# A two-layer hybrid decoder trunk: where weights, replicated rows and transfers are put, and how the planner counts transfers

## The chip, the cores and the metric

One core of one Trainium2 chip runs the whole kernel. The metric is the device time of one launch in microseconds; less is better. The kernel before took 3025.5 us (median of three runs, 3023.38 to 3030.99). The engines are named as the profile names them: PE (TensorE matmul) with PEld (its weight load), DVE (VectorE), ACT (ScalarE), POOL (GpSimd), SP (SyncE). SPq and ACTq are the instruction queues of SyncE and ScalarE seen as issuers of transfers.

## The reference

The input is x, 2048 tokens of 1024 channels, float32. Layer 0 is a gated DeltaNet, layer 1 gated linear attention, each followed by `layer_norm(alpha*x + y)`.

- Gated DeltaNet, 8 heads with 128 key and 256 value channels: one projection of x gives q, k, v, a gate and two logits a head. q, k and v pass a causal convolution over 4 tokens and SiLU, q and k are normalised. In each block of tokens (64 in the reference) a lower triangular system `(A + I) U = [beta*v, beta*k*exp(gc)]` is solved, with `A` the strictly lower part of `beta*k k^T` times a decay. A state of 128 x 256 is then carried from block to block: `v_new = u - w S`, `o = q_dec S + qk v_new`, `S = S*g_last + k_dec^T v_new`.
- Gated linear attention, 4 heads of the same widths: a decay per channel from a low-rank gate, products q k^T with that decay within a block, and a state carried on in the same way.
- Both: the head's output is RMS-normalised, multiplied by `norm_w * silu(gate)`, and goes through an output projection.

## The kernel before, in words

**Staging.** The tokens are cut into 4 groups of 512 (`TG`), and a group into 4 chunks of 128 (`NC`). A unit is one head of one layer for one group: 32 DeltaNet units and 16 units of the second layer, in the order of `PHASES`. Each unit has four stages: `gemms` (input projections), `preps` (decays, products and the triangular solve), `chains` (the state over four chunks), `outs` (output projection, layer norm).

**Weights.** A matmul in full precision is made of three in a reduced format: a float32 weight is split into a high and a low part. `chunk` (line 508) loads a raw block of 128 rows (`wraw`, 6 buffers), ACT copies the high part and POOL subtracts to get the low part, both into a tile `wc` of shape `[P, 2, 272]` with 9 buffers. Units after the second store the split block in device memory (`wk`), and later units load it back with one transfer `wc<-wk`. Most blocks are 256 columns wide, so that the two parts lie 272 elements apart in a partition: two pieces of 1 KB.

**The triangular solve.** `gdn_prep` (line 800) writes the four diagonal 32 x 32 blocks of A of each chunk into `own` (tile `X0`), stores them in device memory, and reads them back replicated: each row of a block is wanted in all the 32 partitions of that block. Two stores, `blk` (all columns) and `blkq` (the first 16 of each 32), are issued by ACT. Then SyncE issues eight loads into `Arep`: four of rows 16 to 31 (256 KB each, one a block of 32 partitions), and four of rows 0 to 15 cut to 16 columns (128 KB each). DVE then goes through the rows from 31 down to 1, two instructions a row (`Xt<-Arep,X` and `X<-X,Xt`, line 861). `Arep` has one buffer.

**Transfers by queue.** SyncE issues all loads and most stores. ACT issues five kinds: `gcT` and `Gb` (the decays of a head, stored and read back in all partitions), `blk`, `blkq`, and `x2T` (the transposed output of layer 0). A transfer instruction is issued in the order of its queue. It counts up one of eight semaphores, numbers 100 to 107 in the trace, that the two queues share: an instruction whose semaphore still belongs to an earlier transfer, on either queue, waits until that one has landed.

**What sets the order.** Nothing is run while it is recorded: `Recorder.note` (line 133) notes each instruction with its dependencies, `cost` (line 183) gives it a busy time and a lag, and `place` (line 234) is a list scheduler. It keeps a clock for each engine, takes the ready instruction of highest priority (chains, preps, early preps, outs, gemms, layer norm, setup; `R_CHAIN` and so on in line 1185), gives out buffers, and so fixes the order of every engine's instructions. `emit` writes them in that order; on the chip each engine follows its list and waits by semaphores. The planned times decide the order alone.

For transfers the planner before has fixed figures: the issue takes 630 ns for `wc` and `wk`, 560 for `wraw`, 430 for `Arep`, 480 for the others, and 340 on ACT; the data is there 3500 ns plus its size at 170 bytes a nanosecond later, 7000 ns for `Arep`, 9500 for `y` and `woraw`. No transfer delays another, apart from the issue time.

Of the kernel before, what the change touches and what calls it, by code (L numbers as in the profile page):

```python
# [7 lines left out]
F32 = mybir.dt.float32  # L8
F32R = mybir.dt.float32r
# [3 lines left out]
ALU = mybir.AluOpType  # L13
# [3 lines left out]
P = 128  # L17
# [3 lines left out]
TG = 512  # L21
NG = SEQ // TG
NC = TG // P
# [84 lines left out]

class Op:
    __slots__ = ("key", "call", "name", "args", "kw", "prio", "cost", "lag", "deps", "users", "waits", "ready",  # L110
                 "views", "fresh", "start", "at", "func", "unit")


def size_of(shape):
# [6 lines left out]
class Recorder:  # L121
# [61 lines left out]
    def cost(self, op, dst, every):  # L183
        key = op.key
        n = size_of(dst.shape)
        psum = any(isinstance(a, View) and a.of.psum for a in every)
        op.func = None
        if key == "t":
            mov = size_of(every[2].shape) if op.name == "matmul" else size_of(every[1].shape)
            if op.name == "transpose":  # L190
                op.cost = 2 * dst.shape[0] / 2.4 + 4
            elif every[1].dtype == F32:
                op.cost = 2 * max(mov / 1.2 + 3, 0.85 * every[1].shape[-1] + 2)
            else:
                op.cost = mov / 2.25 + 4.5
            op.lag = 210
            op.func = op.name == "matmul" and min(dst.shape[0], every[1].shape[0]) < P
        elif key == "d":
            size = 4 * n * dst.shape[0]
            tag = dst.of.tag if isinstance(dst, View) else ""  # L200
            op.cost, op.lag = 630 if tag == "wc" or tag[:2] == "wk" else 560 if tag == "wraw" else 480, DMA_LAG + size / 170
            if tag == "Arep":
                op.cost, op.lag = 430, REP_LAG
            elif tag in ("y", "woraw"):
                op.lag = 9500
        elif key == "a":
            size = 4 * n * dst.shape[0]
            op.cost, op.lag = 340, DMA_LAG + size / 170 + (2500 if isinstance(every[1], View) and every[1].of.tag == "xraw" else 0)
        elif key == "v":
            n = max(n, max(size_of(a.shape) for a in every))  # L210
            took = (150 if psum else 160) + 1.04 * n
            if op.name in ("tensor_reduce", "copy_predicated", "tensor_tensor_scan"):
                took += 1.0 * n
            if op.name != "tensor_tensor" and any(isinstance(a, (View, bass.AP)) and size_of(a.shape) == 1
                                                  for a in every[1:]):
                took += 62 if psum or n < 512 else 85
            op.cost, op.lag = took - 80, 80 + LAG
        elif key == "s":
            took = (165 if psum else 210) + 0.833 * n
            if any(isinstance(op.kw.get(k), (View, bass.AP)) for k in ("scale", "bias")):  # L220
                took += 100 + 67 * ("scale" in op.kw and "bias" in op.kw)
            if "accum_out" in op.kw:
                took += 190
            if op.name == "activation":
                op.func = "ln" if op.args[2] == AF.Ln else None if op.args[2] in (AF.Copy, AF.Square, AF.Identity,
                                                                                 AF.Abs) else "exp"
            op.cost, op.lag = took - 95, 95 + LAG
        else:
            took = 140 + 2.8 * n if len(every) > 2 else 185 + n
            if op.args[-1] == ALU.pow:  # L230
                took = 450 + 160 * n
            op.cost, op.lag = took - 40, 40 + LAG

    def place(self):
# [4 lines left out]
        pending = {e: [] for e in clock}  # L239
# [12 lines left out]
            due[op.unit] += op.prio[0] == R_CHAIN  # L252
        front = 0

        def engine(op):
            return "s" if op.key == "a" else op.key

        def blocked(op):
            for t in op.fresh:
# [4 lines left out]
        def offer(op):  # L264
            tag = "unit" if op.fresh and op.unit > front + HORIZON else blocked(op)
            if tag is not None:
                parked.setdefault(tag, []).append(op)
                return
            ready = op.ready
            for t in op.fresh:  # L270
                ready = max(ready, min(free[t.tag])[0])
            heapq.heappush(pending[engine(op)], (ready, op.prio, op.at))

        def wake(tag):
            for op in sorted(parked.pop(tag, []), key=lambda o: o.prio):
# [6 lines left out]
        while len(placed) < len(self.ops):  # L282
# [16 lines left out]
            if blocked(op) is not None:  # L299
                clock[e] = now  # L300
                offer(op)
                continue
            late = max([0.0] + [min(free[t.tag])[0] for t in op.fresh])
            if late > now:
                heapq.heappush(pending[e], (late, op.prio, op.at))
                continue
# [19 lines left out]
            op.start = now  # L326
            clock[e] = now + cost
            busy[e] += cost
            end = now + cost + op.lag
            placed.append(op)  # L330
            for u in op.users:
                u.ready = max(u.ready, now + cost if u.deps[op] else end - LAG + DRAIN if u.key == op.key == "v" else
# [34 lines left out]
class Recorded:  # L367
# [2 lines left out]

    def __getattr__(self, name):
        def call(*args, also=(), behind=(), **kw):
            key = "a" if self.key == "s" and name == "dma_start" else self.key
            self.recorder.note(self.engine, key, name, args, kw, also, behind)
        return call


LAG, DRAIN = 60, 35
DMA_LAG, REP_LAG, SLACK = 3500, 7000, 100
INSPECT = None  # L380


# [1 line left out]
def trunk(ctx, tc, x, xT, w_in1, conv, a_log, dt_bias, nw1, w_out1, w_in2, gk_up, gk_b, nw2, w_out2,  # L384
# [1 line left out]
    nc = tc.nc  # L386
    rec = Recorder()
    v, s, g = (rec.engine(e, k) for e, k in ((nc.vector, "v"), (nc.scalar, "s"), (nc.gpsimd, "g")))
    pe, sync, acts = rec.engine(nc.tensor, "t"), rec.engine(nc.sync, "d"), s

    def pool(name, bufs=1, space=None):
        kw = {} if space is None else {"space": space}
# [115 lines left out]
    def chunk(spec):  # L508
# [1 line left out]

        w, cols, kc, key = spec
        keep = rec.unit >= N_UNKEPT
        wc = T("wc", [P, 2, 272], W_BUFS, F32R)
        n = sum(2 * cn if pair else cn for c0, cn, pair in cols)
        if key in kept:
            sync.dma_start(wc[:, :, :n].bitcast(F32), kept[key][:])
            return wc
        raw = T("wraw", [P, 272], RAW_BUFS)
        rows = w[kc * P:(kc + 1) * P]
# [8 lines left out]
                n += cn  # L528
        split(wc[:, 0, :n], wc[:, 1, :n], raw[:, :n], g)
        if keep:  # L530
            kept[key] = T("wk", [P, 2, n], p=dr)
            sync.dma_start(kept[key][:], wc[:, :, :n].bitcast(F32))
        return wc

    def load_wo(spec, parts=None):
# [82 lines left out]
    def flat(t):  # L618
        return t.rearrange("p a b -> p (a b)")
# [124 lines left out]
    def gdn_logits(G, gi):  # L744
# [40 lines left out]
        row = T("Gb", [P, TG])[:H1 * NC, :P]  # L785
        s.copy(row, dT)
        rows = T(f"gcT_{gi}", [H1 * NC, P], p=dr)
        acts.dma_start(rows[:], row)
        G.update(beta=beta, ngc=ngc, gdec=gl, eg=eg, rows=rows)

    def later_half(a, sz):
# [8 lines left out]
    def gdn_prep(u):  # L800
        h, G = u.h, u.G
        beta, ngc, eg = G["beta"][:, h, :], G["ngc"][:, h, :], G["eg"]
        Gb = T("Gb", [P, NC, P])
        acts.dma_start(flat(Gb[:]), G["rows"][h * NC:(h + 1) * NC, :].rearrange("a b -> (a b)").unsqueeze(0)
                            .broadcast_to([P, NC * P]))
        D1, D2 = T("D1", [P, NC, P], 2), T("D2", [P, NC, P], 2)
        for n in range(NC):
# [38 lines left out]
        for r0 in range(0, P, 32):  # L846
            r = slice(r0, r0 + 32)
            s.copy(own[r].rearrange("p (n j) -> p n j", n=NC), A[r, :, r])
        late, early = (T(f"{k}_{u.at}", [P, 32 // m * NC], p=dr) for m, k in ((1, "blk"), (2, "blkq")))
        acts.dma_start(late[:], own[:])  # L850
        acts.dma_start(early[:].rearrange("p (n j) -> p n j", n=NC), own[:].rearrange("p (n j) -> p n j", n=NC)[:, :, :16])
        R = T("Arep", [P, 3 * 16 * 16 * NC])
        n = 16 * 32 * NC
        for part, rows, c in ((late, slice(16, 32), slice(0, n)), (early, slice(0, 16), slice(n, 3 * n // 2))):
            for b in range(4):
                sync.dma_start(R[b * 32:(b + 1) * 32, c],
                               part[b * 32 + rows.start:b * 32 + rows.stop, :].rearrange("s n -> (s n)").unsqueeze(0)
                               .broadcast_to([32, c.stop - c.start]))
        X, xt = T("X", [P, NC, 32]), T("Xt", [P, NC, 31])
        g.tensor_copy(X[:], bc(id32[:], 1, NC))  # L860
        for q in range(31, 0, -1):
            w = 32 if q >= 16 else 16
            at = (q - 16) * w * NC if q >= 16 else n + q * w * NC
            row = R[:, at:at + w * NC].rearrange("p (n j) -> p n j", n=NC)[:, :, :q]
            v.tensor_tensor(xt[:, :, :q], row, X[:, :, q:q + 1].broadcast_to([P, NC, q]), ALU.mult)
            v.tensor_tensor(X[:, :, :q], X[:, :, :q], xt[:, :, :q], ALU.subtract)
        v.tensor_tensor(Tm[:].rearrange("p n (b j) -> p n b j", j=32), bc(X[:], 2, 4),
                        bc(C(C_BLK).rearrange("p (b j) -> p b j", j=32), 1, NC), ALU.mult)
# [22 lines left out]
    def gla_prep(u):  # L891
# [13 lines left out]
        kq = u.kq  # L905
        At = T("D2", [P, NC, P], 2)
        b3 = b.rearrange("p (n t) -> p n t", n=NC)
        near = T("Arep", [P, 3 * 16 * 16 * NC])[:, :2 * TG].rearrange("p (n k) -> p n k", n=NC)
        s.copy(near[:, :, :P], kq[:, 1])
        odd = near[:, :, P:P + P // 2]  # L910
        v.tensor_tensor(odd, b3[:, :, 1::2], b3[:, :, 0::2], ALU.subtract)
# [183 lines left out]
    def outs(u):  # L1095
# [40 lines left out]
        if u.last and u.kind == 0:  # L1136
            for kc in range(KC):
                d = PS("g", [P, NC, P])
                xt = T("xraw", [P, TG], X_RAW_BUFS)
                for n in reversed(range(NC)):  # L1140
                    pe.transpose(d[:, n, :], ys[n][:, kc * P:(kc + 1) * P], ident, also=(xt,) if n == NC - 1 else ())
                s.copy(xt[:], flat(d))
                acts.dma_start(x2T[u.gi][:, kc, :], xt[:])

    def load_gb(u, which):
        gb = {}
# [30 lines left out]


PS_BUFS = {"g": 3, "c": 3, "h": 1, "o": 1}
W_BUFS, RAW_BUFS, X_RAW_BUFS = 9, 6, 4  # L1180
WO_BUFS, WO_RAW_BUFS = 2, 2
LN_BUFS = 4
N_WARM = 5
# [46 lines left out]
```

## Time and profile before

| | |
|---|---|
| median of three runs | 3025.5 us |
| profiled execution | 3028.51 us, its span 3026.3 us |
| mean granted clock of TensorE | 0.988 |
| busy: PE, PEld, DVE, ACT, POOL | 97%, 80%, 73%, 41%, 17% of the span |
| transfers | 612.87 MB, mean 203 GB/s |

How to read the rows: a group's row ends with its number, its busy time and mean, and the idle time of the engine ahead of it with what ended it. `A <- B: 20.9, 14, 4.6` among the waits means that A waited for B 20.9 us in total, 14 times, at most 4.6 us. In a row of a stretch, `PE busy (x)` is the busy time with the number of instructions, then follow the granted clock (`PEclk`, 1.00 is full), the mean busy share of the 16 transfer engines, and what they moved. Nearly all rows name line 364, as the planner's `emit` writes all instructions there; the tiles tell them apart.

### The profile page before, as it was taken

How to read it: one execution, taken by the hardware profiler on the slowest of the kernel's cores; microseconds unless marked ns; L12 is line 12 of the kernel's file. 1: busy time of each engine (PE TensorE's matmuls, PEld its weight loads, DVE VectorE, ACT ScalarE, POOL GpSimd, SP SyncE). 2: the span in 40 equal slices, each digit the busy share in tenths (PEclk: the TensorE clock that was granted, in tenths of full speed). 3: DMA queues.
4: the chain of work that ended last, by engine and by line, in shares of the span. 5: the costliest groups of instructions: out<-in, count | busy, mean ns of one | idle time of the engine just before them, and what ended most of it. 6: DMA issues, size and time to landing. Idle time of an engine off the chain costs nothing. (4 is left out here: it accounts for less than half of the span.)

```text
span 3026.3 us, 48052 instructions
## 1 busy us (share of the span) xinstructions
PE 2926.2 (97%) x16172; PEld 2419.0 (80%) x16172; DVE 2201.4 (73%) x5374; ACT 1243.6 (41%) x3233; POOL 499.8 (17%) x848
## 2 busy tenths in 40 slices
PE   8899999999999999999999999999999999999997
PEld 6677777778877887887888888887787888888886
DVE  6878788797777686668778778557787777755655
ACT  5445554543332455333343344333343344433331
POOL 5432444320100233210000000001010000000000
PEclk9999999999999999999999999999999999999998
DMA  6566777695565658687556665768655565857654
GB/s 193 175 196 203 239 234 241 209 293 159 167 182 178 191 165 269 213 286 224 161 163 182 190 207 179 242 228 244 175 171 176 154 193 176 268 192 236 221 183 143
DMA packets 480615, 612.87 MB, mean 203 GB/s; under 512 B 57280, under 2 KB 407744, under 8 KB 464240
## 3 DMA queue, kind: packets, MB, share of 16 engines
q1 hardware_dynamic: 449456, 589.81, 62.9%
q10 hardware_dynamic: 30912, 20.00, 2.4%
q8 instruction: 127, 2.08, 0.3%
q14 instruction: 120, 0.98, 0.1%
HBM read 480.36 MB, written 129.30 MB: 201 GB/s over the span
## 5 line engine op out<-in xcount | busy, mean ns | idle before, releaser
L364 PE MATMUL psg<-xh,wc 128*128 128x512 f32 x3936 | 1349.5, 409 | 29.0 <-DMA wc<-wk 16.3
L364 PEld LDWEIGHTS psg<-xh,wc 128*128 128x128 f32 x3936 | 740.5, 190 | 195.8 <-DMA wc<-wk 20.6
L364 PE MATMUL psg<-xl,wc 128*128 128x512 f32 x1968 | 805.8, 410 | 0.2
L364 PE MATMUL pso<-wo,oth 128*128 128x512 f32 x1472 | 486.1, 406 | 19.1 <-DVE y L364 17.6
L364 PEld LDWEIGHTS psg<-xl,wc 128*128 128x128 f32 x1968 | 374.4, 190 | 76.4 <-DVE xl L364 1.7
L364 DVE SCALAR_TENSOR_TENSOR y<-pso,z,y 128x512 f32<-128x512 f32 x368 | 274.9, 747 | 148.6 <-PE pso L364 127.6
L364 DVE SCALAR_TENSOR_TENSOR acc<-pb,taps,acc 128x512 f32<-128x512 f32 x384 | 300.3, 785 | 76.5 <-ACT acc L364 69.2
L364 POOL TENSOR_TENSOR wc<-wraw,wc 128x256 fp32r<-128x256 f32 (+1 forms) x336 | 283.3, 859 | 423.5 <-ACT wc L364 360.3
L364 PEld LDWEIGHTS pso<-wo,oth 128*128 128x128 f32 x1472 | 263.9, 189 | 82.8 <-DVE y L364 29.0
L364 PE MATMUL pso<-wo,otl 128*128 128x512 f32 x736 | 295.8, 402 | 0.6 <-DVE otl L364 0.6
L364 PE MATMUL psg<-wc,xh 128*128 128x256 f32 (+1 forms) x1344 | 265.3, 289 | 6.2 <-DMA wc<-wk 4.6
L364 DVE TENSOR_TENSOR Xt<-Arep,X 128x124 f32<-128x124 f32 (+30 forms) x992 | 238.6, 241 | 30.6 <-DMA Arep<-blk 7.5
L364 DVE TENSOR_TENSOR X<-X,Xt 128x124 f32<-128x124 f32 (+30 forms) x992 | 242.6, 245 | 23.9
L364 ACT ACTIVATE th<-psg 128x512 f32<-128x512 f32 (+1 forms) x170 | 95.2, 572 | 334.4 <-PE psg L364 315.4
L364 PEld LDWEIGHTS psg<-wc,xh 128*128 128x128 f32 x1344 | 214.6, 189 | 15.0 <-DMA wc<-wk 4.6
L364 PE MATMUL psg<-wc,xl 128*128 128x256 f32 (+1 forms) x672 | 189.4, 287 | 0.0
L364 ACT CAST wc<-wraw 128x256 fp32r<-128x256 f32 (+1 forms) x336 | 126.0, 405 | 116.2 <-DMA wraw<-in_w_in 99.3
L364 PEld LDWEIGHTS pso<-wo,otl 128*128 128x128 f32 x736 | 139.1, 189 | 30.6 <-DVE otl L364 1.6
L364 POOL TENSOR_SCALAR z<-ssq 128x4 f32<-128x4 f32 x44 | 16.8, 383 | 804.7 <-ACT junk L364 804.2
L364 ACT COPY pb<-psg 128x512 f32<-128x512 f32 x128 | 74.8, 585 | 148.4 <-PE psg L364 145.6
L364 POOL COPY halo<-pb 128x3 f32<-128x3 f32 x128 | 35.2, 275 | 577.6 <-ACT pb L364 576.3
L364 PEld LDWEIGHTS psg<-wc,xl 128*128 128x128 f32 x672 | 126.1, 189 | 2.7
(193 smaller groups left out, 4280.3 us busy)
## 6 DMA issues: line engine op xcount, KB each, us to landing
wc<-wk SPq DMA_DIRECT2D x856, 256.0 KB, 3.8
wo<-wok SPq DMA_DIRECT2D x70, 1024.0 KB, 5.0
wk<-wc SPq DMA_DIRECT2D x272, 256.0 KB, 3.0
wraw<-in_w_in SPq DMA_DIRECT2D x336, 128.0 KB, 3.5
Arep<-blk SPq DMA_DIRECT2D x128, 256.0 KB, 5.4
wok<-wo SPq DMA_DIRECT2D x24, 1024.0 KB, 5.3
wc<-wk SPq DMA_DIRECT2D x80, 272.0 KB, 5.3
Arep<-blkq SPq DMA_DIRECT2D x128, 128.0 KB, 6.4
```

Of the source, the lines that this page charges most:

```text
L364: tc.keep_in_program_order(op.call(*[real(a) for a in op.args], **{k: real(a) for k, a in op.kw.items()}))
```

## The change

1. `wc` becomes one row of 544 elements; a block of n columns uses the first 2n, low part right behind the high part. `wk` is the same row in device memory, so that a load or store is one piece a partition (2 KB for 256 columns).
2. `blkq` and the cut rows go. One store `blk`, then four loads, one a block of 32 partitions, each of all 32 rows at full width: 16 KB a partition, 512 KB a load. `Arep` grows from 12 to 16 KB a partition.
3. ACT issues no transfer any more: `gcT`, `Gb`, `blk` and `x2T` are issued by SyncE.
4. The planner's figures for transfers: 430 ns to issue; all pass one pipe that a transfer can enter 900 ns after its issue and that moves 400 bytes a nanosecond; the data is there 2300 ns after (5300 for `y`); and a transfer is issued only when the eighth before it has landed.
5. `wraw` has 5 buffers instead of 6, `xraw` 3 instead of 4.

```diff
@@ Recorder.cost
         elif key == "d":
-            size = 4 * n * dst.shape[0]
-            tag = dst.of.tag if isinstance(dst, View) else ""
-            op.cost, op.lag = 630 if tag == "wc" or tag[:2] == "wk" else 560 if tag == "wraw" else 480, DMA_LAG + size / 170
-            if tag == "Arep":
-                op.cost, op.lag = 430, REP_LAG
-            elif tag in ("y", "woraw"):
-                op.lag = 9500
-        elif key == "a":
-            size = 4 * n * dst.shape[0]
-            op.cost, op.lag = 340, DMA_LAG + size / 170 + (2500 if isinstance(every[1], View) and every[1].of.tag == "xraw" else 0)
+            op.size = 4 * n * dst.shape[0]
+            op.cost, op.lag = 430, DMA_LAG
+            if isinstance(dst, View) and dst.of.tag == "y":
+                op.lag += 3000
@@ Recorder.place
+        pipe, landed = 0.0, [0.0] * LANES
...
-            late = max([0.0] + [min(free[t.tag])[0] for t in op.fresh])
+            late = max([landed[-LANES] if e == "d" else 0.0] + [min(free[t.tag])[0] for t in op.fresh])
...
-            end = now + cost + op.lag
+            if e == "d":
+                pipe = max(pipe, now + cost + DMA_START) + op.size / DMA_RATE
+                landed.append(pipe + op.lag)
+            end = landed[-1] if e == "d" else now + cost + op.lag
...
-DMA_LAG, REP_LAG, SLACK = 3500, 7000, 100
+DMA_START, DMA_LAG, DMA_RATE, LANES, SLACK = 900, 2300, 400, 8, 100
@@ chunk
-        wc = T("wc", [P, 2, 272], W_BUFS, F32R)
         n = sum(2 * cn if pair else cn for c0, cn, pair in cols)
+        both = T("wc", [P, 544], W_BUFS, F32R)[:, :2 * n]
+        wc = both.rearrange("p (a n) -> p a n", a=2)
         if key in kept:
-            sync.dma_start(wc[:, :, :n].bitcast(F32), kept[key][:])
+            sync.dma_start(both.bitcast(F32), kept[key][:])
...
-            kept[key] = T("wk", [P, 2, n], p=dr)
-            sync.dma_start(kept[key][:], wc[:, :, :n].bitcast(F32))
+            kept[key] = T("wk", [P, 2 * n], p=dr)
+            sync.dma_start(kept[key][:], both.bitcast(F32))
@@ gdn_logits, gdn_prep, outs
-        acts.dma_start(rows[:], row)
+        sync.dma_start(rows[:], row)
-        acts.dma_start(flat(Gb[:]), ...
+        sync.dma_start(flat(Gb[:]), ...
-                acts.dma_start(x2T[u.gi][:, kc, :], xt[:])
+                sync.dma_start(x2T[u.gi][:, kc, :], xt[:])
@@ gdn_prep
-        late, early = (T(f"{k}_{u.at}", [P, 32 // m * NC], p=dr) for m, k in ((1, "blk"), (2, "blkq")))
-        acts.dma_start(late[:], own[:])
-        acts.dma_start(early[:]..., own[:]...[:, :, :16])
-        R = T("Arep", [P, 3 * 16 * 16 * NC])
-        n = 16 * 32 * NC
-        for part, rows, c in ((late, slice(16, 32), slice(0, n)), (early, slice(0, 16), slice(n, 3 * n // 2))):
-            for b in range(4):
-                sync.dma_start(R[b * 32:(b + 1) * 32, c],
-                               part[b * 32 + rows.start:b * 32 + rows.stop, :].rearrange("s n -> (s n)").unsqueeze(0)
-                               .broadcast_to([32, c.stop - c.start]))
+        blk = T(f"blk_{u.at}", [P, NC * 32], p=dr)
+        sync.dma_start(blk[:], own[:])
+        R = T("Arep", [P, 32, NC, 32])
+        for r0 in range(0, P, 32):
+            sync.dma_start(R[r0:r0 + 32].rearrange("p s n j -> p (s n j)"),
+                           blk[r0:r0 + 32, :].rearrange("s n -> (s n)").unsqueeze(0).broadcast_to([32, 32 * NC * 32]))
...
         for q in range(31, 0, -1):
-            w = 32 if q >= 16 else 16
-            at = (q - 16) * w * NC if q >= 16 else n + q * w * NC
-            row = R[:, at:at + w * NC].rearrange("p (n j) -> p n j", n=NC)[:, :, :q]
-            v.tensor_tensor(xt[:, :, :q], row, X[:, :, q:q + 1].broadcast_to([P, NC, q]), ALU.mult)
+            v.tensor_tensor(xt[:, :, :q], R[:, q, :, :q], X[:, :, q:q + 1].broadcast_to([P, NC, q]), ALU.mult)
@@ constants
-W_BUFS, RAW_BUFS, X_RAW_BUFS = 9, 6, 4
+W_BUFS, RAW_BUFS, X_RAW_BUFS = 9, 5, 3
```

More of the change, by code (lines that the diff above doesn't have):

```diff
@@ L110 @@
     __slots__ = ("key", "call", "name", "args", "kw", "prio", "cost", "lag", "deps", "users", "waits", "ready",
-                 "views", "fresh", "start", "at", "func", "unit")
+                 "views", "fresh", "start", "at", "func", "unit", "size")
 def size_of(shape):
@@ L253, in place @@
         front = 0
-        def engine(op):
-            return "s" if op.key == "a" else op.key
+        pipe, landed = 0.0, [0.0] * LANES
         def blocked(op):
@@ L271, in offer @@
                 ready = max(ready, min(free[t.tag])[0])
-            heapq.heappush(pending[engine(op)], (ready, op.prio, op.at))
+            heapq.heappush(pending[op.key], (ready, op.prio, op.at))
         def wake(tag):
@@ L372, in call @@
         def call(*args, also=(), behind=(), **kw):
-            key = "a" if self.key == "s" and name == "dma_start" else self.key
-            self.recorder.note(self.engine, key, name, args, kw, also, behind)
+            self.recorder.note(self.engine, self.key, name, args, kw, also, behind)
         return call
 LAG, DRAIN = 60, 35
-DMA_LAG, REP_LAG, SLACK = 3500, 7000, 100
+DMA_START, DMA_LAG, DMA_RATE, LANES, SLACK = 900, 2300, 400, 8, 100
 INSPECT = None
@@ L388, in trunk @@
     v, s, g = (rec.engine(e, k) for e, k in ((nc.vector, "v"), (nc.scalar, "s"), (nc.gpsimd, "g")))
-    pe, sync, acts = rec.engine(nc.tensor, "t"), rec.engine(nc.sync, "d"), s
+    pe, sync = rec.engine(nc.tensor, "t"), rec.engine(nc.sync, "d")
     def pool(name, bufs=1, space=None):
@@ L803, in gdn_prep @@
         Gb = T("Gb", [P, NC, P])
-        acts.dma_start(flat(Gb[:]), G["rows"][h * NC:(h + 1) * NC, :].rearrange("a b -> (a b)").unsqueeze(0)
+        sync.dma_start(flat(Gb[:]), G["rows"][h * NC:(h + 1) * NC, :].rearrange("a b -> (a b)").unsqueeze(0)
                             .broadcast_to([P, NC * P]))
@@ L848, in gdn_prep @@
             s.copy(own[r].rearrange("p (n j) -> p n j", n=NC), A[r, :, r])
-        late, early = (T(f"{k}_{u.at}", [P, 32 // m * NC], p=dr) for m, k in ((1, "blk"), (2, "blkq")))
-        acts.dma_start(late[:], own[:])
-        acts.dma_start(early[:].rearrange("p (n j) -> p n j", n=NC), own[:].rearrange("p (n j) -> p n j", n=NC)[:, :, :16])
-        R = T("Arep", [P, 3 * 16 * 16 * NC])
-        n = 16 * 32 * NC
-        for part, rows, c in ((late, slice(16, 32), slice(0, n)), (early, slice(0, 16), slice(n, 3 * n // 2))):
-            for b in range(4):
-                sync.dma_start(R[b * 32:(b + 1) * 32, c],
-                               part[b * 32 + rows.start:b * 32 + rows.stop, :].rearrange("s n -> (s n)").unsqueeze(0)
-                               .broadcast_to([32, c.stop - c.start]))
+        blk = T(f"blk_{u.at}", [P, NC * 32], p=dr)
[4 more added lines that the diff above has]
+                           blk[r0:r0 + 32, :].rearrange("s n -> (s n)").unsqueeze(0).broadcast_to([32, 32 * NC * 32]))
         X, xt = T("X", [P, NC, 32]), T("Xt", [P, NC, 31])
@@ L907, in gla_prep @@
         b3 = b.rearrange("p (n t) -> p n t", n=NC)
-        near = T("Arep", [P, 3 * 16 * 16 * NC])[:, :2 * TG].rearrange("p (n k) -> p n k", n=NC)
+        near = T("Arep", [P, 32, NC, 32])[:, :8].rearrange("p a n (h k) -> p (a n h k)", h=2).rearrange("p (n k) -> p n k", n=NC)
         s.copy(near[:, :, :P], kq[:, 1])
```

## The prediction

> **What bounds the kernel now.** I read the page's busy times first, then a table of stretches, then the waits of PE and of SyncE's queue.
>
> ```profile
> span 3026.3 us, 48052 instructions
> PE 2926.2 (97%) x16172; PEld 2419.0 (80%) x16172; DVE 2201.4 (73%) x5374; ACT 1243.6 (41%) x3233; POOL 499.8 (17%) x848
> ```
>
> ```profile
> 0.00:625.00 625.00, 579.53 (x2944) 455.82 (x2945) 495.87 (x1172) 313.50 (x879) 253.61 (x371) 0.98 0.71 214
> 1400.00:2080.00 680.00, 679.10 (x3862) 569.42 (x3861) 489.93 (x1233) 263.77 (x680) 48.53 (x118) 1.00 0.63 195
> 2080.00:2125.00 45.00, 36.35 (x154) 28.54 (x153) 31.87 (x86) 12.45 (x31) 3.82 (x9) 0.92 0.80 242
> 2125.00:2800.00 675.00, 673.96 (x3850) 566.73 (x3850) 484.19 (x1225) 260.97 (x654) 46.22 (x106) 1.00 0.63 193
> ```
>
> PE sets the time. It is idle for 100 us (3026.3 - 2926.2): 45 in the first 625 us, while weights are still split, and about 2 in the 1355 us of the second and fourth stretch together. There a transfer can win nothing; it can only lose. Between them lies a short stretch that lost 8.7 us.
>
> ```profile
> PE psg L364 <- DMA wc<-wk: 20.9, 14, 4.6
> PE pso L364 <- DVE y L364: 17.6, 18, 2.8
> SPq L364 <- PE psg L364: 1031.4, 570, 10.3
> SPq L364 <- DMA Arep<-blk: 52.8, 80, 1.8
> SPq L364 <- DMA blk<-X: 33.7, 10, 9.6
> SPq L364 <- DMA Gb<-gcT: 16.8, 3, 8.8
> ```
>
> PE's wait for weights, 20.9 us, is all that transfers cost it directly. SyncE mostly waits for PE to free a `wc`. It also waits for transfers: 52.8 us for the eight replica loads, which take all eight semaphores, and 16.8 for `Gb`, which ACT issues. After a long wait PE's clock falls as well. Four stretches just behind such waits:
>
> ```profile
> 953.00:964.00 11.00, 8.22 (x24) 6.50 (x25) 6.17 (x18) 1.24 (x3) 0.00 (x0) 0.69 0.75 222
> 1374.00:1383.00 9.00, 7.30 (x22) 5.91 (x23) 3.12 (x11) 2.54 (x10) 0.83 (x3) 0.62 0.74 239
> 2096.00:2107.00 11.00, 6.83 (x21) 5.11 (x22) 4.18 (x14) 1.47 (x8) 0.14 (x1) 0.69 0.75 215
> 2841.00:2851.00 10.00, 7.74 (x48) 6.43 (x48) 1.71 (x5) 2.29 (x6) 0.00 (x0) 0.66 0.90 327
> ```
>
> Each loses 3.4 us to the clock (11 x 0.31, 9 x 0.38, 10 x 0.34), 13.6 in all. Weights thus cost 20.9 + 13.6 = 34.5 us: the most that a better order of transfers can bring.
>
> What stands ahead of the third of them? The timelines of SyncE's queue and of PE:
>
> ```profile
> 2086.64 1.94 SPq L364 DMA_DIRECT2D Arep<-blk  x4
> 2088.62 3.89 SPq L364 DMA_DIRECT2D Arep<-blkq  x4
> 2093.50 10.20 SPq L364 DMA_DIRECT2D wc<-wk  x9
> ...
> 2099.64 0.80 PE L364 MATMUL psg<-xh,wc 128*128 128x512 f32 x1 [4.61 <-DMA wc<-wk]
> ```
>
> The replicas of one head. Three such bursts, and a stretch of plain loads without replicas for comparison:
>
> ```profile
> 946.50:953.00 6.50, 6.35 (x34) 5.11 (x32) 5.32 (x9) 3.18 (x12) 1.53 (x2) 1.00 1.00 224
> 1366.00:1372.00 6.00, 6.00 (x27) 4.88 (x26) 5.84 (x9) 1.55 (x3) 0.66 (x2) 1.00 0.99 213
> 2089.50:2096.00 6.50, 5.54 (x24) 4.13 (x22) 5.89 (x10) 1.81 (x3) 0.99 (x1) 1.00 1.00 222
> 2834.00:2841.00 7.00, 6.17 (x47) 5.51 (x46) 4.55 (x14) 2.19 (x5) 0.00 (x0) 1.00 1.05 391
> ```
>
> Replicas keep the transfer engines full (share 1.00) and yet move only 220 GB/s in the mean; plain loads reach 391. So the planner's new figure, 400 bytes a nanosecond, fits plain loads and not replicas.
>
> **The change part by part.** The sum is made against the profiled execution, 3028.5 us (its span and 2.2 around it), 3.0 above the median of the runs.
>
> *Whole replicated rows.* Sizes and issues:
>
> ```profile
> Arep<-blk SPq DMA_DIRECT2D x128, 256.0 KB, 5.4
> Arep<-blkq SPq DMA_DIRECT2D x128, 128.0 KB, 6.4
> wc<-wk SPq DMA_DIRECT2D x856, 256.0 KB, 3.8
> ```
>
> With 32 heads, a head now loads 4 x 256 + 4 x 128 KB = 1.57 MB, 7.1 us at 220 GB/s; after, 4 x 512 KB = 2.10 MB, 9.5 us. Every weight load issued behind it lands 2.4 us later. The planner expects 5.2 us (2.10 MB at 400), so it puts work on PE and DVE that will find its data missing. Fewer, longer pieces could also speed the replicas up, as far as 391 GB/s (5.4 us, a gain of 1.7 a head); I take 220, since the plain loads at 391 have pieces of 1 to 4 KB a partition, no longer than the replicas' 4 and 8.
>
> [...]
>
> What a later weight costs: 9 of the 32 heads come before the first weight load from the store at 624.9 us, so 23 count:
>
> ```profile
> L364 SPq DMA_DIRECT2D Arep<-blk x36: 324/420/1313, 68.4 to 595.0; - x36
> ...
> L364 SPq DMA_DIRECT2D wc<-wk x936: 319/518/1615, 624.9 to 2986.0; - x188
> ```
>
> Bounds: three of the heads above, where PE already waits, pay in full, 7 us; all 23 would pay 55. Because PE lost so little in the long stretches I take 8 heads, 19 us. Clock: where a wait is new, or long, 3.4 us again; none to 23 times (78 us); I take two, 7 us.
>
> *The solve starts later.* DVE's first step needs row 31 of all four blocks: now four 256 KB loads, 1.05 MB (4.8 us); after, all 2.10 MB (9.5 us), 4.7 us more.
>
> ```profile
> DVE Xt L364 <- DMA Arep<-blk: 7.5, 8, 2.1
> ...
> DVE Xt L364 <- DMA Arep<-blk: 1.3, 1, 1.3
> ...
> PE pso L364 <- DVE y L364: 17.1, 16, 2.8
> ```
> ```profile
> 1700.00:1715.00 15.00, 15.00 (x73) 12.27 (x72) 13.08 (x33) 4.56 (x13) 1.41 (x3) 1.00 1.03 287
> ```
>
> The first row is the whole span, the second a stretch from 1704 to 1709, the third the first 625 us. In 8 heads DVE already waits. DVE will wait 8 x 4.7 = 38 to 32 x 4.7 = 150 us. What reaches PE: in the second row's head DVE waited 1.3 us while PE was busy 15.00 of 15.00, so nothing is the lower bound. In the nine early heads, where 17.1 of PE's 17.6 us behind DVE's `y` fall, all 4.7 may: 42 us, the upper. What is late next there is PE's output projection, with one PSUM buffer. I take a quarter, 10 us.
>
> *Side by side.* A `wc` issue of 518 ns falls to about that of a one-piece transfer:
>
> ```profile
> L364 SPq DMA_DIRECT2D wo<-wok x70: 319/326/896, 601.1 to 2916.8; - x70
> L364 ACTq DMA_DIRECT2D Gb<-gcT x32: 325/326/397, 50.4 to 2405.1; - x32
> ```
>
> That frees SyncE of 936 x 0.19 = 180 us. It is hidden: SyncE waits 1031 us for PE's buffers anyway. If that cover went, a burst of nine loads would gain 1.7 us. I take 0, with up to 5 gained. The matmuls and DVE steps keep their shapes.
>
> *All on SyncE.* 32 `Gb`, 32 `blk`, 32 `x2T` and 4 `gcT` cost SyncE 100 x 0.33 = 33 us; 128 replica issues fewer, at 0.42, give back 54. ACT loses 132 issues, 43 us, at 41% busy: 0. New is that a store whose source is late holds up the weight loads behind it, as SyncE's 33.7 us for `blk` do now. Gone is the opposite: SyncE waiting for a semaphore that ACT's transfer holds, up to 8.8 us at once, and four of eight semaphores stay free behind the replicas. The planner knows both now. Bounds: 34.5 us gained, or nothing. Most of the big waits stand behind replicas and keep their bytes, so I take a third, -12. One buffer of `wraw` and `xraw` fewer: 0 to +4, taken as 0; the rule of eight hides it.
>
> Sum: 19 + 7 + 10 - 12 = +24; 3028.5 + 24 = 3052.5, which is 3049.5 against the median. I say **3050 us**, with 3035 to 3085 as this case's own range.
>
> **Rivals.** *Faster, 3003.* One mechanism: SyncE's queue is freed from semaphores that ACT's transfers hold. Its place is behind each burst, where 16.8 us of waiting for `Gb` and 52.8 for replicas now delay the second and later weights; its price is two thirds of 34.5, 23 us. It decides if nine `wc` buffers outlast a burst 2.4 us longer in all but two or three heads. For it: 2 us lost in 1355. Against it: the first weight, not the second, ends the longest wait, and it sits behind the bytes.
>
> *No change, 3025.* The bytes cost 12 and the freed queue brings 12; or the waits change place only.
>
> *Much slower, 3105.* The urgent small transfers, `blk` and `Gb`, stand in one queue behind the bulk. One that is issued behind a burst of 9.5 us lands some 5 us later in the mean than on ACT's own queue; half the heads at 5 us are 80. Against it:
>
> ```profile
> Gb<-gcT ACTq DMA_DIRECT2D x32, 256.0 KB, 3.7
> ```
>
> `Gb` takes 3.7 us to land on ACT's queue, `wc` 3.8 on SyncE's, no longer.
>
> [...]
>
> That the change misses its purpose is small: 512 consecutive elements are one piece a partition by construction.
>
> **How the numbers follow.** Forecast 0.45, faster 0.31, no change 0.17, much slower 0.07. 0.3% is 9 us, about what a measurement of this kernel tells from no change. Faster by more: 0.31; within: 0.17; slower: 0.45 + 0.07 = 0.52. The range takes all of the forecast's case, no change, and the faster case down to 2998; below lies some 0.1, above 3085 the much slower case.
>
> **What would show it.** Right: replica bursts of 9 to 10 us at share 1.00 and 210 to 230 GB/s; DVE's wait for `Arep` up from 7.5 to 40 us or more; PE's wait for `wc` above 35 us; `wc` issues near 330 ns; no wait of SyncE for `Gb` through ACT. Wrong: bursts at 350 GB/s or more, or PE's wait for `wc` under 15 us with DVE's idle time hidden; then the time is near 3003.

## The result, and the profile after

The changed kernel takes 3117.2 us (median of four runs, 3108.1 to 3122.9), the kernel before beside it 3025.7: a ratio of 1.0297, with a 95% interval of 1.0268 to 1.0326. It is 91 us slower. The forecast was 24 us slower, with a range that ended at 3085.

The page of the kernel after, busy times and the replica loads with the time from an issue to its landing:

```profile
span 3106.0 us, 47846 instructions
PE 2945.6 (95%) x16172; PEld 2430.2 (78%) x16172; DVE 2202.0 (71%) x5374; ACT 1241.2 (40%) x3233; POOL 504.8 (16%) x848
...
Arep<-blk SPq DMA_DIRECT2D x128, 512.0 KB, 9.0
```

PE's idle time went from 100 to 160 us. The granted clock fell from 0.988 to 0.981, and 0.007 of 3106 us is another 22 (PE's busy time grew by 19.4 us). Together 82 us; the span grew by 79.7. So the loss is PE waiting, and running slower, as it does just behind a wait in the head below. The two long stretches where PE was hardly idle before, by the same times in the kernel after:

```profile
1400.00:2080.00 680.00, 652.74 (x3656) 543.55 (x3657) 462.63 (x1208) 245.25 (x626) 41.19 (x103) 0.99 0.61 186
2125.00:2800.00 675.00, 648.52 (x3544) 536.12 (x3543) 473.45 (x1220) 254.46 (x655) 49.05 (x117) 0.98 0.64 193
```

They lose 27 and 26 us now, where they lost 0.9 and 1.0. The work has moved within them, though, and each now holds a long wait for weights, or a part of one, whose counterpart stood outside before. Over the same matmuls (counted from the start: 1430.7 to 2144.4 and 2185.8 to 2889.6 us) PE loses 25 and 20 us. What PE waits for in the kernel after, and DVE's wait for the replicas (total, times, longest):

```profile
PE psg L360 <- DMA wc<-wk: 35.2, 12, 6.8
PE pso L360 <- DVE y L360: 29.5, 25, 5.3
PE psh L360 <- DVE S L360: 19.5, 12, 5.2
PE psg L360 <- DVE acc L360: 18.4, 10, 3.9
...
DVE Xt L360 <- DMA Arep<-blk: 112.4, 30, 10.1
```

DVE waits for replicas 112 us instead of 7.5, in 30 heads instead of 8. PE waits 14 us more for weights, and some 43 more for DVE in these three rows (`y` from 17.6 to 29.5, `S` from 2.7 to 19.5, `acc` from 4.5 to 18.4); all its waits for DVE together went from 44 to 91.

One head shows the mechanism. Its timeline in the kernel after: SyncE's queue, DVE, PE.

```profile
2438.69 1.78 SPq L360 DMA_DIRECT2D Arep<-blk  x4
...
2447.34 0.68 DVE L360 TENSOR_TENSOR sq<-psc,cst 128x512 f32<-128x512 f32 x1
2451.30 0.29 DVE L360 TENSOR_TENSOR Xt<-Arep,X 128x124 f32<-128x124 f32 x1 [3.27 <-DMA Arep<-blk]
2451.50 0.75 DVE L360 SCALAR_TENSOR_TENSOR acc<-pb,taps,acc 128x512 f32<-128x512 f32 x1
...
2449.24 0.62 PE L360 MATMUL psg<-xh,wc 128*128 128x512 f32 x2
2452.30 0.55 PE L360 MATMUL psg<-cst,acc 128*128 128x128 f32 x3 [2.44 <-DVE acc L360]
...
2453.82 1.06 PE L360 MATMUL psg<-xh,wc 128*128 128x512 f32 x2
```

The replicas are there 12.6 us after their first issue (2451.30 - 2438.69; 9.2 in the head of before whose issue stands at 2086.64, by the line below). The planner counted 0.43 to issue, 0.9 to start, 5.24 for 2.10 MB and 2.3 to land: 8.9 us, and wrote the first step of the solve at that place in DVE's list. An `acc` that does not need the replicas stands behind it. DVE stalls 3.27 us, `acc` is late, and PE stalls 2.44 us for it. Behind the stall two matmuls of one shape take 1.06 us at a granted clock of 0.50 (2453.8 to 2454.9 us), ahead of it 0.62 at 1.00. The first step of the solve in that head of before:

```profile
2095.81 0.29 DVE L364 TENSOR_TENSOR Xt<-Arep,X 128x124 f32<-128x124 f32 x1 [0.61 <-DMA Arep<-blk]
```

Other heads go the same way, with `S`, `y`, `vt` or `acc` as the late tile: behind 19 of the 30 late first rows PE waits for DVE within 8 us, 48 us in all. In nine of the 30 heads PE was waiting for weights at about that moment.

Two bursts of the kernel after:

```profile
1682.00:1692.00 10.00, 8.55 (x40) 6.70 (x38) 6.47 (x10) 5.07 (x14) 2.16 (x4) 1.00 0.96 202
2441.00:2450.00 9.00, 8.86 (x41) 6.94 (x39) 6.77 (x11) 5.07 (x14) 0.69 (x3) 1.00 0.97 200
```

The longer pieces did not speed the replicas up: 200 to 202 GB/s with the transfer engines full (share 0.96 and 0.97), a little less than the 213 to 224 of before.

### The profile page after: what moved, and what is told of

It reads as the page before. It is cut to its first block, busy times and chain, and to the rows that moved or that the text cites. A ratio compares the mean times of both kernels' runs of the same rounds, so it can differ in the third digit from the quotient of the medians.

```text
span 3106.0 us, 47846 instructions
## 1 busy us (share of the span) xinstructions
PE 2945.6 (95%) x16172; PEld 2430.2 (78%) x16172; DVE 2202.0 (71%) x5374; ACT 1241.2 (40%) x3233; POOL 504.8 (16%) x848
## 5 line engine op out<-in xcount | busy, mean ns | idle before, releaser
L360 PE MATMUL pso<-wo,oth 128*128 128x512 f32 x1472 | 489.8, 409 | 30.2 <-DVE y L360 29.5
L360 DVE SCALAR_TENSOR_TENSOR sg<-th,psg 128x512 f32<-128x512 f32 (+1 forms) x106 | 67.0, 633 | 95.6 <-ACT th L360 93.9
```

What stands on the lines that cost most here:

```text
L360: tc.keep_in_program_order(op.call(*[real(a) for a in op.args], **{k: real(a) for k, a in op.kw.items()}))
```

## The experiments

Three theories stood at the start. A: the replicas land later than planned, and every engine's list has work ahead of its data. B: SyncE's single queue holds weights up. C: a later solve costs, planned or not. Ratios are to the kernel before, run beside each.

### The planner told the replicas' rate

```diff
             op.cost, op.lag = 430, DMA_LAG
+            if isinstance(dst, View) and dst.of.tag == "Arep":
+                op.size *= 2
```

> The changed kernel; only the planner is told that a replica load takes twice its size in the shared pipe (512 KB count as 1 MB, so 200 bytes a nanosecond). The same transfers, bytes and queues; the order of all engines is planned anew. Theory A (the replicas come later than planned: DVE stalls at the first row of the solve, and PE with it): replicas still land 12 to 14 us after their first issue, but DVE's wait for Arep falls from 112 to below 35 us, and the time to 3030 to 3065. Theory B (SyncE's one queue: stores whose source is late hold up weights): as the change, 3100 to 3130. Theory C (the longer solve itself costs, planned or not): DVE's wait falls, but the time stays above 3085.

Measured: 3021.6 us, ratio 0.9984 (0.9968 to 0.9999). The same transfers and bytes, other lists; the whole loss is gone. Its waits:

```profile
DVE Xt L362 <- DMA Arep<-blk: 16.5, 10, 4.5
...
PE psg L362 <- DMA wc<-wk: 9.6, 5, 6.1
```

Theory A holds. B and C fall as the cause of this loss, since the queue is that of the change and so, nearly, is the time from an issue to its landing (9.2 us in the median, 9.0 in the change). The time came out below the expected 3030.

### A margin on top

```diff
+            if isinstance(dst, View) and dst.of.tag == "Arep":
+                op.size, op.lag = 2 * op.size, DMA_LAG + 3000
```

> The changed kernel; a replica load counts twice in the pipe and is expected 3000 ns later still, so that the solve is planned 17.3 us after the first issue, later than nearly all landings (12 to 17 us). If only work planned ahead of its data costs: DVE's wait for Arep below 6 us, time 3005 to 3022, no worse than with the plan at 14.2 us. If a later solve costs by itself: above 3030.

Measured: 3023.8 us, ratio 0.9981 (0.9970 to 0.9991), and DVE's wait for replicas is 0.7 us, once. A solve planned 3 us later still costs nothing that can be seen. The time is just above the expected range, and level with the run without margin.

### Replicas alone, and the weights behind them alone

With the rate wrong, two things are late: the replicas, and the weights behind them in the pipe. Two runs put each right by itself.

```diff
-                op.size *= 2
+                op.lag += 5240
```

> The changed kernel; the planner expects the replicas 5240 ns later (the solve is planned 14 us after the first issue), but lets them through the shared pipe at 400 bytes a nanosecond as in the change, so that the weights behind them are still planned some 4 us too early. If the solve that starts too early on paper is the loss: DVE's wait for Arep below 35 us, time 3015 to 3045. If the late weights are it: PE's wait for wc stays at 30 us or more, time 3070 or more.

```diff
-                op.size *= 2
+                op.size, op.lag = 2 * op.size, max(DMA_LAG - 5240, -2800)
```

> The converse: the planner lets a replica load take twice its size in the pipe, so that the weights behind are planned right, but expects the replicas themselves as early as the change did (the solve planned 9 us after the first issue). If the solve is the loss: DVE's wait for Arep 90 us or more, time 3085 to 3125. If the weights are it: 3020 to 3050.

Measured: 3080.5 us (1.0162, 1.0142 to 1.0182) with the replicas alone right, 3150.9 us (1.0391, 1.0370 to 1.0412) with the weights alone right. The first run lies where the late weights were expected to show; the second shows the expected wait of DVE, with a time above its range. Neither error is the loss alone. The waits, first with the replicas right:

```profile
DVE Xt L362 <- DMA Arep<-blk: 5.9, 5, 2.0
...
PE psg L362 <- DMA wc<-wk: 36.1, 14, 6.2
```

and with the weights right:

```profile
DVE Xt L362 <- DMA Arep<-blk: 130.8, 29, 11.4
...
PE psg L362 <- DVE vt L362: 30.3, 9, 6.2
PE pso L362 <- DVE y L362: 26.1, 26, 4.3
PE psh L362 <- DVE S L362: 23.5, 8, 6.5
PE psg L362 <- DVE acc L362: 17.6, 9, 8.3
PE psg L362 <- DMA wc<-wk: 5.6, 3, 4.8
```

| ratio to before | weights planned right | weights planned early |
|---|---|---|
| replicas planned right | 0.9984 | 1.0162 |
| replicas planned early | 1.0391 | 1.0297 |

Each error brings its own wait. With the weights planned early PE waits 36 us for `wc`, against 9.6 with both right. With the replicas planned early it waits 141 us for DVE in all, against 65. The errors do not add: replicas early alone cost 1.0391 - 0.9984, 4.1% or 123 us, both together 3.1%. A likely reason is that the two waits often fall together, as in the nine heads of the change where PE was waiting for weights when the replicas were late; no run shows this by itself.

### Every fourth partition

These two kernels leave out the right placing of the blocks, so they serve to measure and not to compute. In the planner's recorder, a load that steps over partitions counts as one that may touch all of `Arep`. The first try therefore made each of the four loads wait for the one before.

```diff
-            sync.dma_start(R[r0:r0 + 32].rearrange("p s n j -> p (s n j)"),
+            sync.dma_start(R[r0 // 32::4].rearrange("p s n j -> p (s n j)"),
```

> The changed kernel, instruction for instruction in the same order; only the 32 partitions that a replica load writes are every fourth one (0, 4, 8 ... and so on for the other three loads) and not 32 neighbours. This leaves out the right placing of the blocks: the solve runs on mixed rows, so the values differ; the work and its order do not. Theory A with the destination partitions as the cause of 220 GB/s: the bursts move 350 GB/s or more, replicas land 8 to 9 us after the first issue as planned, DVE's wait for Arep below 20 us, time 3025 to 3055. If reading the same rows 32 times is the cause: bursts stay at 220 GB/s and the time at 3117. Theory B: bursts faster, time still above 3090.

Measured: 3012.1 us, ratio 0.9955 (0.9938 to 0.9972). The order was not that of the change, as the text had it: the loads ran one after another, and the planner knew. It counted four times 0.43 + 0.9 + 1.3 + 2.3, about 20 us, and DVE waited this long:

```profile
DVE Xt L360 <- DMA Arep<-blk: 6.1, 6, 1.5
```

So the run says nothing on partitions by itself. On theory C it says that even a solve planned 20 us after the first issue does not bring the loss: the time is below that of the kernel before. It is not shown to be free, as the next run, with the same partitions and an earlier solve, is 0.6% faster. The second try gives each stepped load its own part in the recorder; the lists and waits of all engines are then those of the change.

```diff
-            return (0, P, 0, 1 << 20)
+            return (0, P, 0, 1 << 20) if ap[0][0] != 4 * pitch else (32 * (off // pitch), 32 * (off // pitch) + 32, ...)
```

> The change with the same instructions, order and waits on every engine; a replica load writes every fourth partition (0, 4, 8 ..., the next load 1, 5, 9 ...) and not 32 neighbours, and the planner is told that the four do not meet. The blocks are not where the solve wants them, so that the values differ. If the destination's partitions hold the rate at 220 GB/s: bursts at 350 GB/s or more, all four landed about 8 to 9 us after the first issue, as planned; DVE's wait for Arep below 15 us; time 3005 to 3040. If it is the reading of the same rows 32 times: landed after 12 to 14 us, time 3105 to 3125.

Measured: 2997.0 us, ratio 0.9891 (0.9869 to 0.9913). Two bursts, one head's first issue, and DVE's wait:

```profile
933.00:939.00 6.00, 6.00 (x30) 4.94 (x30) 5.76 (x10) 3.47 (x6) 0.36 (x2) 1.00 0.96 342
992.00:998.00 6.00, 6.00 (x30) 4.92 (x29) 5.76 (x10) 3.55 (x6) 0.45 (x1) 1.00 0.93 331
...
930.51 2.36 SPq L360 DMA_DIRECT2D Arep<-blk  x4
939.91 0.29 DVE L360 TENSOR_TENSOR Xt<-Arep,X 128x124 f32<-128x124 f32 x1
...
DVE Xt L360 <- DMA Arep<-blk: 17.2, 8, 6.8
```

With the very same lists these bursts move 331 to 342 GB/s instead of 200, a load lands 6.3 us after its issue in the median instead of 9.0, the solve shown starts 9.4 us after the first issue, and 120 us go. The partitions that these loads write set their rate; reading the same rows 32 times does not. The bursts shown stayed below the expected 350 GB/s and DVE's wait 2 us above the expected 15, while the time came out below its range.

### Replicas from two queues

```diff
-            sync.dma_start(R[r0:r0 + 32].rearrange("p s n j -> p (s n j)"),
+            (sync, other)[r0 // 64].dma_start(R[r0:r0 + 32].rearrange("p s n j -> p (s n j)"),
```

where `other` issues on ACT and is planned in SyncE's stream.

> The change with two of the four replica loads (blocks 2 and 3, partitions 64 to 127) issued by ACT instead of SyncE; planned as before in one stream. If the two halves of the partitions are the two halves of the way into SBUF: both run side by side, a burst moves 350 GB/s or more, all landed 8 to 10 us after the first issue, DVE's wait for Arep below 30 us, time 3015 to 3050 (ACT may stall on the wait for blk in its own order). If not: landed after 12 to 14 us and 3100 or more.

Measured: 3123.5 us, ratio 1.0311 (1.0286 to 1.0335), no better than the change; DVE's wait for replicas is 118.4 us in 30 heads. The issues of one head:

```profile
1396.69 0.78 SPq L360 DMA_DIRECT2D Arep<-blk  x2
1396.75 0.81 ACTq L360 DMA_DIRECT2D Arep<-blk  x2
```

Loads to the two halves of the partitions, issued at the same time from two queues, were no faster: a load landed 9.5 us after its issue in the median, against 9.0 in the change. Why two halves side by side do not reach the rate of every fourth partition, no run here shows.

### The cut rows back

The changed kernel with the replicas of before (two stores, eight loads of 1.57 MB), all on SyncE; then the same with the rate told.

```diff
-        blk = T(f"blk_{u.at}", [P, NC * 32], p=dr)
+        late, early = (T(f"{k}_{u.at}", [P, 32 // m * NC], p=dr) for m, k in ((1, "blk"), (2, "blkq")))
...
-        R = T("Arep", [P, 32, NC, 32])
+        R = T("Arep", [P, 3 * 16 * 16 * NC])
```

> The changed kernel with the replicas of the kernel before: two stores blk and blkq, eight loads with the cut rows, 1.57 MB a head, all issued by SyncE and planned with the shared pipe. Theory A: the first four loads land about 8 us after the first issue where the plan has some 6.5; DVE's wait for Arep 30 to 60 us, time 3050 to 3080. Theory B: 3100 to 3130, since the queue is as in the change (with eight loads instead of four, rather slower). C: about 3030.

> The replicas of the kernel before, all issued by SyncE, and the planner told that a replica load takes twice its size in the pipe. Theory A: the plan is right now, DVE's wait for Arep below 20 us, time 3020 to 3045, level with the kernel before. Theory B: 3095 to 3130.

Measured: 3046.5 us (1.0070, 1.0054 to 1.0087), and 3021.4 us (0.9987, 0.9976 to 0.9997). The first time is 4 us below its expected range, the second within its own. Fewer bytes, of which the first step needs only those of the first four loads, take away most of the loss. What is left is again the rate, as DVE's wait shows: 40.0 us in 22 heads without it and 19.9 in 5 with it.

### Whole rows in the kernel before

```diff
-        late, early = ...
+        blk = T(f"blk_{u.at}", [P, NC * 32], p=dr)
+        acts.dma_start(blk[:], own[:])
...
-W_BUFS, RAW_BUFS, X_RAW_BUFS = 9, 6, 4
+W_BUFS, RAW_BUFS, X_RAW_BUFS = 9, 5, 3
```

> The kernel before with whole replicated rows in four loads alone (one store blk, issued by ACT as before), and the 5 and 3 buffers that make room for it; its planner, its two queues and its weights' layout stay, with 7000 ns as the replicas' lag. Theory A (replicas later than planned is the whole loss): landed 12 to 14 us after the first issue against a plan of 8.8, DVE's wait for Arep 80 to 130 us, time 3085 to 3125. If the loss needs the new planner or the one queue: below 3060.

Measured: 3177.5 us, ratio 1.0490 (1.0468 to 1.0512), with 105.0 us of DVE's wait, as expected, and a time far above the expected 3125. It is worse than the change, so the other parts of the change, the new planner among them, together win some 60 us. With a right lag:

```diff
-DMA_LAG, REP_LAG, SLACK = 3500, 7000, 100
+DMA_LAG, REP_LAG, SLACK = 3500, 11000, 100
```

> The kernel before with whole replicated rows in four loads and 5 and 3 buffers, as the run with 3177 us, but the replicas' lag in its planner 11000 instead of 7000 ns: the solve is planned 12.8 us after the first issue. If the lateness against the plan is the loss there too: DVE's wait for Arep from 105 to below 40 us, time 3030 to 3070. If the old planner loses by something else (fewer buffers, weights planned without a shared pipe): above 3100.

Measured: 3147.3 us, ratio 1.0370 (1.0340 to 1.0401). DVE's wait fell to 36.4 us, as expected, the time far less than expected. The waits:

```profile
DVE Xt L364 <- DMA Arep<-blk: 36.4, 15, 5.9
...
PE psg L364 <- DMA wc<-wk: 65.1, 25, 9.3
```

The old planner lets no transfer delay another, so it counts on the weights behind a burst too early; PE waits 65 us for them, 33 in the run before. That is the wait of the second error in the table again, though no run sets that error right in the old planner.

### The weights' parts alone

Part 1 of the change in the kernel before, with the planner's figures and so all lists as they were.

> The kernel before with the weights' parts side by side alone; the planner's figures and so the order of every engine stay as they were. The issue of a weight load falls from 518 to about 328 ns and its packets from 1 to 2 KB. If that is hidden: 3018 to 3032. If the refill behind a burst gains by it: PE's wait for wc falls from 20.9 to below 15 us, time 3005 to 3018.

Measured: 3016.7 us, ratio 0.9953 (0.9939 to 0.9967). The issue row:

```profile
L364 SPq DMA_DIRECT2D wc<-wk x936: 319/320/2336, 623.6 to 2983.9; - x188
```

518 ns became 320. The runs gain 14 us, which is in the second range of the expectation without its sign: PE's wait for `wc` is 19.9 us against 20.9, and the profiled span is only 4 us shorter. The place of the gain stays open.

### The buffers

```diff
-W_BUFS, RAW_BUFS, X_RAW_BUFS = 9, 6, 4
+W_BUFS, RAW_BUFS, X_RAW_BUFS = 9, 5, 3
```

> The kernel before with 5 buffers of wraw and 3 of xraw instead of 6 and 4, all else the same. Whole rows alone cost the kernel before 147 us with these buffers, the whole change 91. If the buffers are the difference: 3060 to 3090. If the planner without a shared pipe is it: 3020 to 3045 here.

Measured, in the kernel before: 3047.2 us, ratio 1.0052 (1.0035 to 1.0070), 16 us; far from the 147 of whole rows. Its waits:

```profile
PE psg L364 <- ACT wc L364: 19.8, 9, 3.9
```

PE waits 19.8 us for ACT's part of the split, 4.0 before. The time lies just above the lower of the two expected ranges. Last, the changed kernel with cut rows, the rate told, and the old number of buffers, for which the smaller `Arep` leaves room:

> The changed kernel with the cut rows of before, replicas counted twice in the pipe (3021 us), and 6 and 4 buffers again, for which the smaller Arep leaves room. If the buffers matter: 3000 to 3015, which would beat both kernels. If not: 3016 to 3028.

Measured: 3007.2 us, ratio 0.9919 (0.9904 to 0.9934). It beats both kernels, and by the ratios it is 0.7% faster than the same kernel with 5 and 3 buffers (0.9987). PE's wait for weights, 5.7 us there, is nearly gone:

```profile
PE psg L362 <- DMA wc<-wk: 2.9, 7, 0.7
```

## Why the prediction was right or wrong

**Right: the direction and its mechanism.** The forecast took the replicas at 220 GB/s and 9.5 us where the planner took 5.2, and named what would be late: the first row of the solve, and the weights behind. Bursts are full at 200 to 202 GB/s (210 to 230 was named), DVE's wait rose to 112 us (40 or more was named as the sign, 38 to 150 as the bounds), and PE's wait for weights to 35.2 (above 35 was named). `wc` issues take 320 ns, as said. The run with every fourth partition shows that this one rate is worth 120 us.

**Wrong: what of DVE's wait reaches PE.** This is the step that failed: "I take a quarter, 10 us", between bounds of nothing and 42. PE waits 43 us more behind DVE in three rows, 47 in all, which is above the upper bound. Two errors are in it. That a wait of 1.3 us left PE busy was read as slack for longer ones; in the head shown of the kernel after, 2.44 of 3.27 us reach PE, by an instruction that stands behind the solve in DVE's list. And such a loss was allowed for in the nine early heads alone; it came in the long stretches as well.

**Wrong in size: the clock.** The term was 7 us, for two new waits; the fall of the granted clock is worth some 22. PE's waits of 3 us or more rose from 2 to 13, which fits, but no run changes the clock by itself.

**Too low: the weights.** The sum had 19 us for later weights and -12 for the single queue, 7 together; PE's wait for weights grew by 14. Nothing measured the queue alone. With replicas and weights planned right that wait is 9.6 us, 11 below the kernel before, so a gain near 12 is there, but it comes with the shared pipe in the planner. Weights planned early then add 26, not 19.

With the measured 14, 47 and 22 the sum gives 83 us; the span grew by 79.7.

**Wrong in two terms that nearly cancel.** One buffer fewer of `wraw` and `xraw` was taken as 0, with 4 as its bound: it costs 16 us in the kernel before, and "the rule of eight hides it" had no row behind it. The weights' parts side by side were taken as hidden, with 5 at most: they gain 14 us there. That the two nearly cancel is luck.

**The rivals.** The faster case had its condition wrong: the nine buffers of `wc` do not outlast the longer burst while the planner does not count it. Once the planner did, PE's wait for weights fell by 11 us, but the time by 5 and not by 23. The much slower case gave a time near the measured one, 3105, by luck, as no run supports its mechanism: the small transfers stand in SyncE's queue in all runs with the rate told, which are level with the kernel before or faster. The 5 us that it put on a transfer behind a burst are shown by no run: `Gb` landed 3.6 us after its issue on SyncE's queue in the change and 3.7 on ACT's before, `blk` 1.5 and 1.8 (medians).

## What to carry to other kernels

In a kernel whose instruction lists are fixed by a planner, a transfer's planned time must not be too short: here a burst planned some 4 us too early, 32 times, cost 3%, while a solve planned 3 us later than its true rate asks cost nothing that could be seen. Measure each shape of transfer on the chip, by rate and by time to land, and put that into the plan; one rate for all failed here, where the replicas moved 200 to 202 GB/s and were planned at 400. When asking what a stall costs, look at what stands behind the stalled instruction in its engine's list and who waits for that; a stall of 1.3 us that was absorbed said nothing about one of 3.

## What was not expected of the hardware

In the bursts shown, the replica loads to 32 neighbouring partitions moved 200 to 224 GB/s with the transfer engines full (share 0.96 to 1.00); those to every fourth partition, with the bytes and pieces of the change, 331 to 342 (share 0.93 and 0.96). Issuing the two halves from two queues did not help (1.0311 against 1.0297). The issue of a `wc` load, mostly 256 KB, took 320 ns in one piece a partition and 518 in two (medians).
